# Hybrid trunk on one core: the first norm's squares summed on TensorE, v's last pass by chunks, the meta product over 128 rows, and other matmul costs in the planner

## The chip, the core and the metric

The kernel runs on one core of a Trainium2 chip. A core has a matrix engine (TensorE; PE in the profile, its weight loads PEld), a vector engine (VectorE, DVE), a scalar engine (ScalarE, ACT), a general engine (GpSimd, POOL) and SyncE (SP), whose queue issues the DMAs here. The metric is the device time of one execution in microseconds; less is better.

## The reference

A decoder trunk of two layers over 528 tokens of width 1024: 16 learned meta tokens, then 512 tokens of the input. Each layer is, cut to what the change touches:

```python
xn = rms_norm(h, norm1_g[l])          # h * rsqrt(mean(h*h) + 1e-6) * g
proj = xn @ w_in[l]
z, xbc, dt_raw, q, k, v, gate_logits = jnp.split(proj, split_at, axis=-1)
y_ssd = ssd_mixer(z, xbc, dt_raw, ...)           # dt = softplus(dt_raw + dt_bias); chunks of 128
y_attn = sliding_window_attention(q, k, v, ...)  # 16 q heads, 4 kv heads of 64
merged = g_ssd * (y_ssd @ w_ssd_down[l]) + g_attn * (y_attn @ w_attn_down[l])
h = h + merged @ w_o[l]
hn = rms_norm(h, norm2_g[l])
h = h + jnp.square(jax.nn.relu(hn @ w_mlp_up[l])) @ w_mlp_down[l]
```

In the attention each block of 128 queries sees a window of 128 keys, all 16 meta tokens and a sink logit: `out = probs[..., :16] @ v_meta + probs[..., 16:] @ v_band`. The states of the SSD decay by `exp(cumsum(dt * a))`. All inputs are 32-bit floats, and the meta tokens are dropped from the output.

## The kernel before

**Layout.** The activations `h` lie with the 1024 features on partitions, as eight tiles (`KD` = 8) of 128 features by 528 tokens; the tokens are cut into five `CHUNKS`, of which chunk 0 holds the meta tokens. Every large product is made in three passes over numbers split in two, in a type of which TensorE takes a column at a time: weights into `whi` and `wlo` (ACT casts `whi`, POOL subtracts to get `wlo`, some of it DVE), activations into `hnh` and `hnl` (`hgh` and `hgl` in layer 1, where the norm's factor is put in later). The passes are high by high, low by high and high by low. Small products (sums over partitions, transposes, broadcasts) are made with plain 32-bit operands; TensorE's records show two of them for each.

**The start.** The eight tiles of `h`, the constants `cst` and the first weights are loaded. For the first norm ACT squares tile after tile, DVE adds all but the last square up in `acc`, and TensorE sums `acc` and the last square over the partitions with a column of ones: five chunks by two, ten products of 128 by 1 into one bank (`rms_tok`, from L592). DVE scales the sums, POOL raises them to the power of -1/2 (`rt`), TensorE broadcasts `rt` to all partitions (`bcast_tok`), DVE multiplies `h` by it, ACT and DVE make `hnh` and `hnl`. The later norms use the same functions.

**v and dt.** The first projection makes v (256 columns) and dt (32) together, 288 columns with the tokens as rows: five banks, one for each chunk, weights `wvh` and `wvl` (`WideWeights`, from L448). The first two passes go row by row (tile k by `wvh`, all five chunks, then the low part of the tile before); the last is

```python
for k in range(KD):
    v_row(k, 2, stop=k == KD - 1)      # wvl: for every k, all five chunks
```

so all five banks are finished together. Then each chunk is evicted in turn: `dtx` (DVE), the high part of v (ACT), the low part (DVE), into `vm` for the meta tokens and `vt` for the rest. `vm` is 64 rows: 32 rows, of which 16 count, and a copy of them. `dt_task` (L757) follows: a chain of 2 operations of ACT and 15 of DVE on 128 by 160 (`scr`, `dtx`, `dtt`) makes softplus and then `adt`, which TensorE sums along the tokens (`cst,adt`).

**Attention.** For each group of four heads and block of queries the scores are made, the largest taken (`mx`), exponentials and their sum made, and then `piece` (L1064) runs for each piece of the keys: TensorE transposes the probabilities (`cst,at`, L434), ACT copies them as the high part into `ar`, DVE subtracts to get the low part, and TensorE multiplies both by v. For the meta tokens high and low part are stacked in 64 rows, 32 each, so that there is one product of 64 by 512 (`ar,vm`); the other pieces take two of 128 by 512 (`ar,vt`).

**What sets the order.** The program is written out by a planner, `Flow` (L124). Tasks are generators in queues (weights, post, misc, chunk, attn, tail and others); each yields where it waits for data, a bank, or TensorE. The planner keeps a clock for every engine, adds to it the estimated cost of each instruction that it emits (`Engine.cost` for DVE, ACT and POOL, `mm` for TensorE), and between the large products (`tick`) lets those tasks step whose needs are met by its own clocks. The order so found is fixed for each engine; semaphores hold it at run time. For the matmuls the estimate is:

```python
if rhs.dtype == F32R and n >= 256:
    cost = n / 2.4
else:
    cost = max(n, 128) * 4 / 2.4 * (0.66 if o.shape[0] == 64 else 1.0)
```

`F.force` steps tasks until the given ones are done; `F.finish` and `F.step` move single tasks on. The conversion of v's first weights (the casts to `wvh` on ACT) is such a task, and was stepped twice, which issues the loads. There are eight banks of PSUM (`ps`), and two buffers each of `raw`, `xh`, `sq` and `zs`.

Of the kernel before, what the change touches and what calls it, by code (L numbers as in the profile page):

```python
# [9 lines left out]
F32 = mybir.dt.float32  # L10
F32R = mybir.dt.float32r
# [6 lines left out]
P = 128  # L18
# [288 lines left out]
class Engine:  # L307
# [12 lines left out]
    def cost(self, name, n, k, aps):  # L320
        scalars = sum(isinstance(k.get(x), bass.AP) for x in ("scalar", "scale", "bias", "mul"))
        if self._k == "v":
            if name == "reciprocal":
                return 6.4 * n + 60.0
            if name == "tensor_tensor_reduce":
                return n / 0.96 + 165.0
            return n / 0.96 + 62.0 + (58.0 if scalars else 0.0)
        if self._k == "s":
            psum = any(x.space == PSUM for x in aps)
            return n / 1.2 + (48.0 if psum else 86.0) + 93.0 * scalars + (95.0 if "accum_out" in k else 0.0)  # L330
        if k.get("op") == ALU.pow:
            return 190.0 * n + 120.0
        if name == "memset":
            return 40.0
        return n * (2.09 if name == "tensor_tensor" else 3.8) + 125.0
# [19 lines left out]
def hybrid_trunk_kernel(ctx: ExitStack, tc: tile.TileContext, h0, params, consts, rope, wdt, w, out,  # L355
# [69 lines left out]
    def mm(o, lhsT, rhs, start=True, stop=True):  # L425
        n = Engine.size(rhs)
        if rhs.dtype == F32R and n >= 256:
            cost = n / 2.4
        else:
            cost = max(n, 128) * 4 / 2.4 * (0.66 if o.shape[0] == 64 else 1.0)  # L430
        F.run("pe", cost, [o], [lhsT, rhs], PE.matmul(out=o, lhsT=lhsT, rhs=rhs, start=start, stop=stop))  # L431
# [160 lines left out]
    def rms_tok(sq, inv_n, cs, tag, rows=(), bank="ps"):  # L592


        yield {bank: 1, "after": rows, "data": lambda: [x[:, CHUNKS[cs[0]][0]:sum(CHUNKS[cs[-1]])] for x in sq()]}
        ps = Slot("ps")
        for c in cs:
            t0 = CHUNKS[c][0]
            x = sq()
            for i in range(len(x)):  # L600
                mm(ps.t[:, c:c + 1], x[i][:, t0:t0 + P], C("ones"), start=i == 0, stop=i == len(x) - 1)
# [3 lines left out]
        V.tensor_scalar(out=x, in0=ps.t[:, cs[0]:cs[-1] + 1], scalar1=inv_n, scalar2=EPS, op0=ALU.mult, op1=ALU.add)  # L605
        ps.free()
# [68 lines left out]
    for x, q in ((wt[0, "v", 0], "w"), (wt[0, "v", 1], "w"), (wvt.dt, "misc")):  # L675
        assert x in tasks_
        F.step(x, F.queues[q])
        F.step(x, F.queues[q])
# [4 lines left out]
    acc = Slot("zs", "acc")  # L683
    for k in range(KD):
        sq = Slot("sq") if k else acc
        S.activation(out=sq.t, in_=h(k), func=AF.Square)
        if k == KD - 1:
            nrm["sq"] = sq
        elif k:
            V.tensor_tensor(out=acc.t, in0=acc.t, in1=sq.t, op=ALU.add)  # L690
            sq.free()
    first.append(F.put("misc", norm(acc, 0, (), keep=True)))
    F.force(first)
    F.end = 0.0

    for l in range(depth):
# [130 lines left out]
        vm = lay.tile([64, NKV, 2, 64], F32R, name="vm", tag="vm")  # L827
# [6 lines left out]
        def v_row(k, x, start=False, stop=False):  # L834
            for c in range(5):
                t0 = CHUNKS[c][0]
                mm(banks[c].t[:, 0:wvt.N], (src.lo if x == 1 else src.hi)(k)[:, t0:t0 + P], wvt(1 if x == 2 else 0, k),
                   start=start, stop=stop)
# [8 lines left out]
        for k in range(KD):  # L847
            v_row(k, 2, stop=k == KD - 1)
        F.finish(*first)
        del first[:]  # L850
        for c in range(5):
            ps = banks[c]
            F.end = 0.0
# [148 lines left out]
        def attention(n, kv):  # L1002
# [61 lines left out]
            def piece(p):  # L1064
# [10 lines left out]
                if kk < P <= nq:  # L1075
# [12 lines left out]
                    mm(po[0].t[:, :4 * nq], vm[:, kv].rearrange("p x d -> p (x d)"), ar[0:64, h_],  # L1088
# [62 lines left out]
        ar = unit("ar", F32R).rearrange("p r t -> p (r t)")  # L1151
        put_attention(qt, 0)
# [571 lines left out]
```

## Time and profile before

| | |
|---|---|
| time of three runs, median (lowest to highest) | 2446.96 us (2444.26 to 2449.26) |
| time of the profiled execution | 2436.77 us |
| its span, first to last instruction | 2435.1 us |
| granted TensorE clock, mean over the span | 0.992 |
| busy: TensorE, DVE, ACT, POOL | 2363.5, 1337.1, 1025.4, 1097.8 us (97, 55, 42, 45% of the span) |
| moved by DMA | 257.33 MB, 106 GB/s on average |

The profiled execution lies 10.2 us under the median of the three timed ones and 7.5 us under the fastest. Times in the trace count from the span's start. TensorE's matmuls overlap, and the end of each is modelled, so what one costs in a row of like ones is read from the distance of two starts (the pitch), not from its length. [...] In brackets behind a row stands the engine's idle time before it, and who ended it.

### The profile page before, as it was taken

To read this page: it belongs to the slowest core of one execution; us is meant where nothing else is said; L and a number is where in the kernel's file an instruction comes from. 1 tells how busy PE (TensorE), PEld (TensorE's weight loads), DVE (VectorE), ACT (ScalarE), POOL (GpSimd) and SP (SyncE) were. 2 spreads that over 40 slices of the span, in tenths; PEclk is the share of its full clock that TensorE was granted. 3 is DMA by queue.
4 is the path that set the end of the run, shared out by engine and by line. 5 is a ranking of instruction groups with operands and counts; after the bars stand their busy time and mean duration, and the time that the engine had idled before them with its cause. 6 is when DMAs were issued, how large, how long until landed. Compare 5 with 4: busy or idle time off the path is not lost.

```text
span 2435.1 us, 40407 instructions
## 1 busy us (share of the span) xinstructions
PE 2363.5 (97%) x16038; PEld 2143.3 (88%) x16038; DVE 1337.1 (55%) x2509; ACT 1025.4 (42%) x1999; POOL 1097.8 (45%) x651
## 2 busy tenths in 40 slices
PE   6999999999999999999999899999999999999999
PEld 6889899999999999999997788888988788888887
DVE  5787788787522444233246868787875135433221
ACT  4365566564432233222244456556554223333231
POOL 3534434465444334343434454445555543444443
PEclk9999999999999999999999999999999999999999
DMA  4323333343443322222232233324434533222222
GB/s 138 91 75 106 83 102 93 90 116 101 118 177 113 141 79 87 96 87 96 94 136 82 69 100 105 106 73 121 118 93 133 177 121 135 89 95 95 95 95 104
DMA packets 133578, 257.33 MB, mean 106 GB/s; under 512 B 16470, under 2 KB 66318, under 8 KB 133390
## 3 DMA queue, kind: packets, MB, share of 16 engines
q1 hardware_dynamic: 133390, 254.75, 33.4%
q8 instruction: 127, 2.08, 0.3%
q14 instruction: 61, 0.50, 0.1%
HBM read 232.03 MB, written 17.33 MB: 102 GB/s over the span
## 4 chain that ended last, share of the span: by engine, by line
PE 80%; DVE 12%; issue 3%; ACT 2%; POOL 2%; DMA 1%; SPq 0%; DVEq 0%; POOLq 0%; ACTq 0%
PE ps L431 78%; PE ps L434 2%; DVE xb L348 2%; DVE at L348 1%; DVE raw L348 1%; DVE xh L348 1%; DVE rqs L348 1%; DVE scr L348 1%; DVE gm L348 1%; POOL wlo L348 1%; DVE ar L348 1%; DVE mx L348 1%; DMA gm<-ac_dram 0%; DVE qa L348 0%; ACT at L348 0%
## 5 line engine op out<-in xcount | busy, mean ns | idle before, releaser
L348 POOL TENSOR_TENSOR wlo<-wraw,whi 128x1024 fp32r<-128x1024 f32 x328 | 797.5, 2431 | 982.7 <-ACT whi L348 930.4
L348 ACT CAST whi<-wraw 128x1024 fp32r<-128x1024 f32 x340 | 355.5, 1046 | 707.5 <-PE ps L431 421.4
L431 PE MATMUL ps<-hnh,whi 128*128 128x266 f32 (+2 forms) x2048 | 401.2, 312 | 5.3 <-DVE vm L348 4.6
L431 PE MATMUL ps<-hnl,whi 128*128 128x266 f32 (+2 forms) x2048 | 399.3, 311 | 0.0
L431 PE MATMUL ps<-hnh,wlo 128*128 128x266 f32 (+2 forms) x2048 | 391.8, 308 | 0.0
L431 PEld LDWEIGHTS ps<-hnh,whi 128*128 128x128 f32 x2048 | 307.2, 192 | 20.6 <-issue 6.8
L431 PEld LDWEIGHTS ps<-hnl,whi 128*128 128x128 f32 x2048 | 307.7, 192 | 15.1 <-issue 1.3
L431 PEld LDWEIGHTS ps<-hnh,wlo 128*128 128x128 f32 x2048 | 304.0, 190 | 15.2 <-issue 2.3
L348 DVE SCALAR_TENSOR_TENSOR h<-ps,h 128x264 f32<-128x264 f32 (+1 forms) x120 | 62.1, 517 | 308.8 <-PE ps L431 308.8
L348 DVE TENSOR_TENSOR hidl<-s,hidh 128x528 fp32r<-128x528 f32 (+1 forms) x64 | 116.9, 1827 | 88.1 <-ACT s L348 88.1
L431 PE MATMUL ps<-hgl,whi 128*128 128x264 f32 (+1 forms) x768 | 153.7, 322 | 1.3 <-DVE hgl L348 1.3
L431 PE MATMUL ps<-hgh,wlo 128*128 128x264 f32 (+1 forms) x768 | 153.4, 321 | 0.0
L431 PE MATMUL ps<-hgh,whi 128*128 128x264 f32 (+1 forms) x768 | 152.8, 321 | 0.0
L431 PE MATMUL ps<-hidl,whi 128*128 128x264 f32 (+1 forms) x768 | 152.6, 321 | 0.0
L431 PE MATMUL ps<-hidh,whi 128*128 128x264 f32 (+1 forms) x768 | 152.5, 320 | 0.0
L431 PE MATMUL ps<-hidh,wlo 128*128 128x264 f32 (+1 forms) x768 | 152.5, 320 | 0.0
L431 PE MATMUL ps<-y,whi 128*128 128x264 f32 (+1 forms) x768 | 137.0, 320 | 0.0
L431 PEld LDWEIGHTS ps<-hgl,whi 128*128 128x128 f32 x768 | 119.0, 188 | 12.4 <-DVE hgl L348 1.6
L431 PEld LDWEIGHTS ps<-hgh,wlo 128*128 128x128 f32 x768 | 119.5, 189 | 11.0
L431 PEld LDWEIGHTS ps<-hidl,whi 128*128 128x128 f32 x768 | 118.9, 188 | 11.0
L431 PEld LDWEIGHTS ps<-hidh,wlo 128*128 128x128 f32 x768 | 118.8, 188 | 11.0
L431 PEld LDWEIGHTS ps<-hidh,whi 128*128 128x128 f32 x768 | 118.7, 188 | 11.1
(218 smaller groups left out, 3947.5 us busy)
## 6 DMA issues: line engine op xcount, KB each, us to landing
wraw<-w_dram SPq DMA_DIRECT2D x344, 512.0 KB
gm<-ac_dram SPq DMA_DIRECT2D x64, 256.0 KB
et<-ac_dram SPq DMA_DIRECT2D x128, 64.0 KB
t<-au SPq DMA_DIRECT2D x48, 66.0 KB
h<-h_dram SPq DMA_DIRECT2D x8, 264.0 KB
at<-rope_dram SPq DMA_DIRECT2D x4, 528.0 KB
y_dram<-xb SPq DMA_DIRECT2D x4, 528.0 KB
yr<-y_dram SPq DMA_DIRECT2D x8, 264.0 KB
```

What stands on the lines that cost most here:

```text
L348: inst = fn(*a, **k)
L431: F.run("pe", cost, [o], [lhsT, rhs], PE.matmul(out=o, lhsT=lhsT, rhs=rhs, start=start, stop=stop))
L434: F.run("pe", 108.0 if in_.shape[1] > 64 else 60.0, [o], [in_], PE.transpose(out=o, in_=in_, identity=C("ident", k)[:, :k]))
```

## The change

1. **The first norm's sums.** DVE adds nothing up any more. Each of the eight squares goes to TensorE as it is made: five products of 128 by 1 for each, 40 instead of ten, into five banks. The squares take turns in four kinds of buffer. The five sums are then scaled on DVE one by one. The casts to `wvh` are stepped on right behind the norm. ACT's order at the start of the program, before (`acc` is the buffer of the first square and of the sum):

```order
L348 ACTIVATE acc<-h_80 128x528
L348 ACTIVATE sq<-h_80 128x528 x3
L348 ACTIVATE sq<-h_81 128x528 x4
L348 ACTIVATE hnh_154<-h_80,par 128x528 x2
L348 CAST wvh<-wraw 128x7x128
L348 CAST wvh_93<-wraw 128x128
L348 CAST wvh<-wraw 128x7x128
L348 CAST wvh_93<-wraw 128x128
L348 CAST wvh<-rawdt 128x7x32
L348 CAST wvh_93<-rawdt 128x32
L348 ACTIVATE hnh_154<-h_80,par 128x528 x2
```

And after:

```order
L350 ACTIVATE sq<-h_80 128x528 x4
L350 ACTIVATE sq<-h_81 128x528 x4
L350 CAST wvh<-wraw 128x7x128
L350 CAST wvh_93<-wraw 128x128
L350 CAST wvh<-wraw 128x7x128
L350 CAST wvh_93<-wraw 128x128
L350 CAST wvh<-rawdt 128x7x32
L350 CAST wvh_93<-rawdt 128x32
L350 ACTIVATE hnh_192<-h_80,par 128x528 x4
L350 ACTIVATE hnh_193<-h_81,par 128x528
```

The casts to `wvh` stood behind the first two `hnh` and stand ahead of them now.

2. **v's last pass by chunks.** The products with `wvl` run chunk by chunk, eight for each, and each chunk's eviction follows its own. 40 products before, 40 after. `vm` becomes 128 rows, the upper 64 filled with zeros by POOL once a layer.

3. **The meta product.** It reads 128 rows of `ar` and `vm` instead of 64; the upper rows of both `ar` buffers are filled with zeros by POOL, once a layer. The products of the 16-row meta block stay as they were.

4. **The planner's costs.** A large product counts n/2.25 + 4 ns instead of n/2.4 (121 instead of 110 for 264 columns), a small one n * 4/2.28 instead of n * 4/2.4, a product with an output of 64 rows 0.9 of that instead of 0.66; on DVE the product with a running maximum (`tensor_tensor_reduce`) counts 25 ns more, and a `tensor_scalar` without PSUM about half. This moves instructions on all engines. On TensorE in layer 0, in the large products for k and q that follow v, around the decay's first sums (`cst,adt`), before:

```order
L431 MATMUL ps<-hnh_155,wlo 128x264 x2
L431 MATMUL ps<-hnh_154,whi 128x264 x4
L431 MATMUL ps<-cst,adt 32x128 x4
L431 MATMUL ps<-hnh_155,whi 128x264 x2
L431 MATMUL ps<-hnl_156,whi 128x264 x4
L431 MATMUL ps<-hnl_157,whi 128x264 x2
L431 MATMUL ps<-cst,au 128x2 x5
L431 MATMUL ps<-hnh_154,wlo 128x264 x2
L431 MATMUL ps<-cst,adt 32x16
L431 MATMUL ps<-adt,cst 16x32
```

And after:

```order
L433 MATMUL ps<-hnl_195,whi 128x264 x2
L433 MATMUL ps<-hnh_193,wlo 128x264 x2
L433 MATMUL ps<-hnh_192,whi 128x264 x4
L433 MATMUL ps<-hnh_193,whi 128x264 x2
L433 MATMUL ps<-hnl_194,whi 128x264 x4
L433 MATMUL ps<-hnl_195,whi 128x264 x2
L433 MATMUL ps<-hnh_192,wlo 128x264 x2
L433 MATMUL ps<-cst,adt 32x128 x4
L433 MATMUL ps<-hnh_192,wlo 128x264 x2
L433 MATMUL ps<-hnh_193,wlo 128x264 x2
```

The decay's `cst,adt` stood behind the 124th large product after v (of 264 columns) and five sums `cst,au`; it stands behind the 62nd now. In the attention of layer 1 the same holds for a group of probabilities. TensorE, the 79th of 92 groups, from its transposes to its product with v, before:

```order
L434 MATMUL ps<-cst,at_14821 128x128 x4
L431 MATMUL ps<-hnl_14181,whi 128x512 x4
L431 MATMUL ps<-xdd,btk 128x256
L431 MATMUL ps<-hnl_14182,whi 128x512 x2
L434 MATMUL ps<-cst,xb 128x128 x3
L431 MATMUL ps<-xb 128x128
L431 MATMUL ps<-hnh_14179,wlo 128x512 x4
L431 MATMUL ps<-hnh_14180,wlo 128x512 x2
L431 MATMUL ps<-hnh_14180,whi 128x512 x2
L431 MATMUL ps<-hnl_14182,whi 128x512 x2
L431 MATMUL ps<-hnh_14180,wlo 128x512 x2
L431 MATMUL ps<-ar,vt 128x512 x2
```

And after:

```order
L436 MATMUL ps<-cst,at_14856 128x128 x4
L433 MATMUL ps<-hnl_14218,whi 128x266 x2
L433 MATMUL ps<-hnl_14219,whi 128x266 x2
L433 MATMUL ps<-hnh_14216,wlo 128x266 x4
L433 MATMUL ps<-hnh_14217,wlo 128x266 x2
L433 MATMUL ps<-hnh_14217,whi 128x266 x2
L433 MATMUL ps<-hnl_14219,whi 128x266 x2
L433 MATMUL ps<-hnh_14217,wlo 128x266 x2
L433 MATMUL ps<-hnh_14216,whi 128x266 x2
L433 MATMUL ps<-ar,vt 128x512 x2
```

Between the transposes and the product stood 18 products of 512 columns and five smaller instructions, and there stand 18 of 266 columns now. Over all 92 groups the distance shrinks in more than half and grows in the others. Over the whole program DVE takes 21 subtractions of the split of q instead of 8, and POOL 15 instead of 28.

The diff, cut:

```diff
@@ -323,7 +323,9 @@
...
             if name == "tensor_tensor_reduce":
-                return n / 0.96 + 165.0
+                return n / 0.96 + 190.0
+            if name == "tensor_scalar" and not any(x.space == PSUM for x in aps):
+                return n / 1.92 + 62.0 + (58.0 if scalars else 0.0)
             return n / 0.96 + 62.0 + (58.0 if scalars else 0.0)
...
@@ -425,9 +427,9 @@
     def mm(o, lhsT, rhs, start=True, stop=True):
         n = Engine.size(rhs)
         if rhs.dtype == F32R and n >= 256:
-            cost = n / 2.4
+            cost = n / 2.25 + 4.0
         else:
-            cost = max(n, 128) * 4 / 2.4 * (0.66 if o.shape[0] == 64 else 1.0)
+            cost = max(n, 128) * 4 / 2.28 * (0.9 if o.shape[0] == 64 else 1.0)
...
@@ -589,21 +591,25 @@
-    def rms_tok(sq, inv_n, cs, tag, rows=(), bank="ps"):
-        yield {bank: 1, "after": rows, "data": lambda: [x[:, CHUNKS[cs[0]][0]:sum(CHUNKS[cs[-1]])] for x in sq()]}
-        ps = Slot("ps")
-        for c in cs:
-            t0 = CHUNKS[c][0]
-            x = sq()
-            for i in range(len(x)):
-                mm(ps.t[:, c:c + 1], x[i][:, t0:t0 + P], C("ones"), start=i == 0, stop=i == len(x) - 1)
+    def rms_tok(sq, inv_n, cs, tag, rows=(), bank="ps", sums=None):
+        if not sums:
+            yield {bank: 1, "after": rows, "data": lambda: [x[:, CHUNKS[cs[0]][0]:sum(CHUNKS[cs[-1]])] for x in sq()]}
+            ps = Slot("ps")
+            for c in cs:
+                t0 = CHUNKS[c][0]
+                x = sq()
+                for i in range(len(x)):
+                    mm(ps.t[:, c:c + 1], x[i][:, t0:t0 + P], C("ones"), start=i == 0, stop=i == len(x) - 1)
         yield
         r = sm.tile([P, 5], F32, name=tag, tag=tag)
         x = r[:, cs[0]:cs[-1] + 1]
-        V.tensor_scalar(out=x, in0=ps.t[:, cs[0]:cs[-1] + 1], scalar1=inv_n, scalar2=EPS, op0=ALU.mult, op1=ALU.add)
-        ps.free()
+        for c in cs if sums else (cs[0],):
+            y, z = (x[:, c:c + 1], sums[c].t[:, 0:1]) if sums else (x, ps.t[:, c:cs[-1] + 1])
+            V.tensor_scalar(out=y, in0=z, scalar1=inv_n, scalar2=EPS, op0=ALU.mult, op1=ALU.add)
+        for z in sums or (ps,):
+            z.free()
@@ -672,7 +678,8 @@
...
-    for x, q in ((wt[0, "v", 0], "w"), (wt[0, "v", 1], "w"), (wvt.dt, "misc")):
+    v_tasks = ((wt[0, "v", 0], "w"), (wt[0, "v", 1], "w"), (wvt.dt, "misc"))
+    for x, q in v_tasks:
         assert x in tasks_
         F.step(x, F.queues[q])
         F.step(x, F.queues[q])
@@ -680,17 +687,30 @@
...
-    acc = Slot("zs", "acc")
+
+    sums = [Slot("ps") for _ in CHUNKS]
     for k in range(KD):
-        sq = Slot("sq") if k else acc
+        sq = Slot(min(("zs", "sq", "xh", "raw"), key=lambda n: F.rings[n].at()), "sq")
         S.activation(out=sq.t, in_=h(k), func=AF.Square)
-        if k == KD - 1:
-            nrm["sq"] = sq
-        elif k:
-            V.tensor_tensor(out=acc.t, in0=acc.t, in1=sq.t, op=ALU.add)
-            sq.free()
-    first.append(F.put("misc", norm(acc, 0, (), keep=True)))
+        for c in range(5):
+            t0 = CHUNKS[c][0]
+            mm(sums[c].t[:, 0:1], sq.t[:, t0:t0 + P], C("ones"), start=k == 0, stop=k == KD - 1)
+        F.end = F.t["pe"]
+        sq.free()
+
+    def first_norm():
+        nrm["rt"] = yield from rms_tok(None, 1.0 / D, range(5), "rt", sums=sums)
+        nrm["banks"] = []
+        for x in bcast_tok(nrm["rt"], range(5), "bank"):
+            if isinstance(x, dict):
+                yield x
+            else:
+                nrm["banks"].append(x)
+
+    first.append(F.put("misc", first_norm()))
     F.force(first)
+    for x, q in v_tasks:
+        F.step(x, F.queues[q])
...
@@ -824,18 +844,18 @@
...
-        vm = lay.tile([64, NKV, 2, 64], F32R, name="vm", tag="vm")
+        vm = lay.tile([P, NKV, 2, 64], F32R, name="vm", tag="vm")
+        G.memset(vm[64:128].bitcast(F32), 0.0)
         rtm = sm.tile([32, 1], F32, name="rtm", tag="rtm")
         rows_, src = (made, hg) if l else (normal, hn)
         F.force(rows_[:2])
         F.finish(wvt.dt, wt[l, "v", 0], wt[l, "v", 1])
         banks = [Slot("ps") for _ in CHUNKS]
 
-        def v_row(k, x, start=False, stop=False):
+        def v_row(k, x, start=False):
             for c in range(5):
                 t0 = CHUNKS[c][0]
-                mm(banks[c].t[:, 0:wvt.N], (src.lo if x == 1 else src.hi)(k)[:, t0:t0 + P], wvt(1 if x == 2 else 0, k),
-                   start=start, stop=stop)
+                mm(banks[c].t[:, 0:wvt.N], (src.lo if x else src.hi)(k)[:, t0:t0 + P], wvt(0, k), start=start, stop=False)
                 F.tick()
 
         for k in range(KD + 1):
@@ -844,12 +864,14 @@
                 v_row(k, 0, start=k == 0)
             if k:
                 v_row(k - 1, 1)
-        for k in range(KD):
-            v_row(k, 2, stop=k == KD - 1)
         F.finish(*first)
         del first[:]
         for c in range(5):
             ps = banks[c]
+            for k in range(KD):
+                t0 = CHUNKS[c][0]
+                mm(ps.t[:, 0:wvt.N], src.hi(k)[:, t0:t0 + P], wvt(1, k), start=False, stop=k == KD - 1)
+                F.tick()
             F.end = 0.0
...
@@ -1085,7 +1107,7 @@
...
-                    mm(po[0].t[:, :4 * nq], vm[:, kv].rearrange("p x d -> p (x d)"), ar[0:64, h_],
+                    mm(po[0].t[:, :4 * nq], vm[:, kv].rearrange("p x d -> p (x d)"), ar[:, h_],
                        start=(p == 0), stop=(p == len(pieces) - 1))
...
@@ -1149,6 +1171,8 @@
 
         at2 = unit("at2").rearrange("p r t -> p (r t)")
         ar = unit("ar", F32R).rearrange("p r t -> p (r t)")
+        for i in range(2):
+            G.memset(ar[64:128, i * 1024:i * 1024 + 512].bitcast(F32), 0.0)
```

## Rows read from the trace of the kernel before

**Rows 1.** The page, part 1: each engine's busy time, share, instructions

```profile
PE 2363.5 (97%) x16038; PEld 2143.3 (88%) x16038; DVE 1337.1 (55%) x2509; ACT 1025.4 (42%) x1999; POOL 1097.8 (45%) x651
```

**Rows 2.** Waits, TensorE: who waited <- for whom: total us, times, longest

```profile
PE ps L431 <- DVE ar L348: 17.2, 15, 2.3
...
PE ps L431 <- DVE mx L348: 6.5, 1, 6.5
```

**Rows 3.** Chain that ended last, 0 to 30 us: start, length, what

```profile
5.31 5.00 DMA cst<-consts_dram
...
24.57 2.36 ACT wvh L348 x5
...
26.97 3.25 PE ps L431 x12
```

**Rows 4.** Timeline, 13 to 46 us: start, length, engine, operation; TensorE, then ACT

```profile
14.98 0.56 PE L431 MATMUL ps<-cst,acc 128*128 128x1 f32 x2
...
17.97 0.57 PE L431 MATMUL ps<-cst,sq 128*128 128x1 f32 x2
...
31.93 1.38 PE L431 MATMUL ps<-wvh,hnl 128*128 128x288 f32 x5
...
33.13 0.83 PE L431 MATMUL ps<-wvh,hnh 128*128 128x288 f32 x5
...
40.45 5.45 PE L431 MATMUL ps<-wvl,hnh 128*128 128x288 f32 x40
...
23.16 1.41 ACT L348 ACTIVATE hnh<-h,par 128x528 fp32r<-128x528 f32 x2 [8.67 <-DVE h L348]
```

**Rows 5.** Busy time by stretch (window, its length, each engine, clock)

```profile
core 0: us, PE busy (x) PEld busy (x) DVE busy (x) ACT busy (x) POOL busy (x), PEclk, DMA share, GB/s
879.66:883.07 3.41, 3.41 (x31) 3.41 (x32) 0.17 (x1) 0.00 (x0) 1.03 (x1) 1.00 0.43 153
883.07:886.49 3.42, 3.42 (x17) 3.15 (x16) 0.02 (x1) 0.39 (x1) 0.15 (x1) 0.50 0.00 0
```

**Rows 6.** Timeline inside the first stretch, TensorE: the last of ten sums

```profile
881.40 0.36 PE L431 MATMUL ps<-cst,sq 128*128 128x1 f32 x2
```

**Rows 7.** Timeline of layer 0's decay chain: DVE, POOL, TensorE

```profile
49.95 0.18 DVE L348 TENSOR_TENSOR dtx<-ps,par 128x32 f32<-128x32 f32 x1
...
51.46 0.24 DVE L348 TENSOR_SCALAR scr<-scr 128x160 f32<-128x160 f32 x1 [0.46 <-ACT scr L348]
...
52.93 2.87 DVE L348 TENSOR_TENSOR scr<-scr 128x160 f32<-128x160 f32 x2
...
64.78 0.32 DVE L348 TENSOR_TENSOR adt<-dtt,na 128x160 f32<-128x160 f32 x1
...
53.22 2.39 POOL L348 TENSOR_TENSOR wlo<-wraw,whi 128x1024 fp32r<-128x1024 f32 x1 [13.33 <-ACT whi L348]
...
65.16 1.06 PE L431 MATMUL ps<-cst,adt 128*32 128x128 f32 x8 [3.06 <-DVE adt L348]
```

**Rows 8.** Timeline of one attention step, TensorE

```profile
1368.92 0.50 PE L431 MATMUL ps<-ar,vm 64*128 64x512 f32 x1 [2.25 <-DVE ar L348]
...
1369.35 0.66 PE L434 MATMUL ps<-cst,at 128*128 128x128 f32 x4
...
1371.70 0.62 PE L431 MATMUL ps<-ar,vt 128*128 128x512 f32 x2
...
1372.16 0.41 PE L431 MATMUL ps<-hnh,whi 128*128 128x266 f32 x2
```

**Rows 9.** Timeline, layer 1's first norm and first k product, TensorE

```profile
1264.43 0.36 PE L431 MATMUL ps<-cst,acc 128*128 128x1 f32 x2
...
1265.99 0.36 PE L431 MATMUL ps<-cst,sq 128*128 128x1 f32 x2
...
1268.25 1.03 PE L431 MATMUL ps<-cst,rt 16*128 16x16 f32 x6
...
1280.11 1.00 PE L431 MATMUL ps<-hnh,whi 128*128 128x264 f32 x3 [4.57 <-DVE vm L348]
```

## The prediction

> **What bounds the kernel now.** I read the page's busy shares first: TensorE is busy for 2363.5 of 2435.1 us, the next engine for 1337.1 [rows 1]. So there are two ways to win: fewer or cheaper matmuls, or less of the roughly 72 us in which TensorE stands still. The waits of TensorE came second: it waited 17.2 us in 15 places for DVE's half of the split probabilities (`ar`), and once 6.5 us for the largest score of an attention group [rows 2]. Third, the chain of the start: until 10.31 us the constants are under way, and ACT's casts of v's weights (24.57 to 26.93) stand directly ahead of the first v product at 26.97 [rows 3]. The same stretch of the timeline shows that TensorE runs there at the lower of its two speeds: five v products take 1.20 us (31.93 to 33.13), and later 40 take 5.45 [rows 4].
>
> The profiled execution took 2436.77 us, 1.67 more than its span; I sum against it, and add the result to the median of 2446.96, which lies 10.2 us higher.
>
> **The change part by part.**
>
> *The start.* Removed from the path: six adds on DVE. Added: 30 more sums on TensorE. Eight sums are 2.99 us apart there (14.98 to 17.97, seven distances), 0.427 us each [rows 4]. The sums need the constants, which land at 10.31 [rows 3]; 40 of them last until 27.4, against 18.5 before: 8.9 us later. Behind them comes the same chain (scale, power, broadcast, multiply) to the first `hnh`, which ACT began at 23.16 and ended after half of 1.41 us, at 23.9 [rows 4]; now 32.8. But the casts to `wvh` no longer follow on that: ACT runs them while TensorE sums, so the first v product starts there and not after them. 32.8 against 26.97 is **+5.9 us**. One DVE operation became five small ones, which I count as nothing, because the distance of two small operations there is hidden in my rounding to 0.1 for each, at most +0.5. In the other direction the speed may rise sooner, since TensorE has worked longer: of the 25 v products that ran at 0.24 us before 33.13 half would then take 0.136, a gain of 1.3. Range +4.6 to +6.4.
>
> [...]
>
> *v's last pass by chunks.* The 40 products remain, at 0.136 us. What moves is the eviction. Before, v ends at 45.9, the five evictions follow on DVE and ACT, the last `dtx` starts at 49.95, and the decay chain's DVE part starts at 51.46, 5.6 us behind v [rows 4, 7]. Now four evictions run beside the products of the next chunks, and the chain starts 1.5 us (49.95 to 51.46) after the last one, so at about v's end + 1.6. The chain is 15 DVE operations: the first two take 1.47 us (51.46 to 52.93), the other 13 between 0.24 and 0.32 each when nothing disturbs (the first and the last of the chain), at most 4.2 us [rows 7]. So `adt` is ready at v's end + 7.3. Its first sums stand behind 62 large products instead of 124 and five sums: 62 times 0.125 (0.136 by 264 of 288 columns, an estimate) is 7.7 us. They would just not wait, where before they waited 3.06 us at 65.16 [rows 7]. I take **-2.8**. The other end: two operations of the chain took 2.87 us instead of 0.64 while POOL made a weight's low half from 53.22 on, and the whole chain took 13.6 us (51.46 to 65.10) [rows 7]. With that price in full, `adt` is ready at v's end + 15.2, and TensorE waits 7.5 us: +4.5. POOL's subtraction began 7.3 us behind v's end; the chain now ends about there. That is why I choose the undisturbed end, and why the other one is a rival. Low end -3.1.
>
> *The meta product.* 32 products of 64 rows by 512 columns. One starts 0.43 us ahead of what follows (1368.92 to 1369.35), a product of 128 rows with the same 512 columns 0.23 (1371.70 to 1372.16, two) [rows 8]. Taking the shape of the latter, each saves 0.20: **-6.3**. The upper rows are zeros and are written by POOL once a layer, three fills on an engine that is idle for more than half of the span [rows 1]. No row shows such a fill; the nearest, a subtraction of 128 by 1024, takes POOL 2.39 us [rows 7], and a fill has a quarter to a half of its elements. The weights' second buffer hides it; without that cover a layer would lose up to 2.4 us once. High end 0, if rows had nothing to do with it. [...] The two rows differ by a factor of 1.9, so the measurement decides.
>
> *Layer 1's entry.* There the planner, whose products are now dearer by a tenth, puts the norm's ten sums behind 49 products of v and no longer behind 63. TensorE then waits 4.57 us for a bank that only `vm`'s eviction frees, at 1280.11, and that eviction stands on DVE behind the rows that wait for the norm [rows 9]. Fourteen products of 0.136 us are 1.9 us by which the norm starts earlier in the same work. The chain from the sums to the broadcast (1266.2 to 1268.25) is covered by v products as before [rows 9]. I take **-1.6**, from 0 to -4.6, the whole wait.
>
> *The order in the attention.* The new costs make TensorE slower in the planner's book, by a tenth for large products, and DVE faster for copies, so it believes an `ar` to be ready after fewer products. Counting the work that stands on TensorE between a group's transposes and its product with v, at the pitches above, the median of 92 groups falls from 3.9 to 2.9 us, and those under 2.5 us rise from 18 to 32. A fixed latency of 2.6 us, beyond which each missing microsecond is waited for, gives 17.3 us before, which is what the waits show [rows 2], and 25.6 with the new order: +8.3. But DVE's and ACT's queues move with it: where the work came close, DVE was often late because of something else queued ahead. I take half, **+4**. Ends: +15 with a latency of 2.9 us (37.8 less 23.4, rounded up) and -5, if the 6.5 us pause [rows 2] falls to 1.5 in the new order and nothing else changes. In the order the products ahead of that pause are as many as before, so I let it stand.
>
> Thirteen subtractions of q's split go from POOL to DVE, which is 45% idle [rows 1]; nothing, or part of the last term.
>
> **Sum:** +5.9 - 2.8 - 6.3 - 1.6 + 4 = -0.8 us. 2436.8 becomes 2436.0; 2446.96 becomes **2446**.
>
> **The rivals.**
>
> 1. *The order costs nothing.* The groups that moved closer were ones whose DVE work was early, and the pause shrinks: the last part is -5 instead of +4, the sum -9.8, the time 2437. For it speaks that only 15 of 92 groups waited although 18 had less than 2.5 us; against it that the new order more than doubles the groups under 2.9 us (23 to 46).
> 2. *The sums raise the clock.* If 17 us of sums bring TensorE to the upper level, a sum costs 0.223 us as in layer 1 (1264.43 to 1265.99, seven distances) [rows 9]: 40 times 0.204 is 8.2 us less, and the first 25 v products save 2.6. Sum -11.6, 2435. Against it stands the stretch from 879.66 [rows 5].
> 3. *Slower: the decay chain meets POOL's subtraction.* If that starts 2 us earlier in the new order (ACT's casts are sooner done) or v's last eviction is late by as much, seven or more of the chain's operations run at several times their length. The price is 7.3 over my value, the sum +6.5, 2453.5. It decides from about 5 us behind v's end. For it: rows 7 show this very chain disturbed.
> 4. *Slower: the dense attention is paid in full,* by the latency of 2.9 us: +15 instead of +4, the sum +10.2, 2457.
> 5. *The meta product gains nothing,* because its time has another reason than its rows: sum +5.5, 2452.5.
>
> **How the numbers follow.** What a measurement of this kernel can tell from no change is about 0.2%, 4.9 us: 2442.1 to 2451.9. My forecast, 2446 with a range of its own from 2442 to 2451, has 0.34. Faster: rival 1 has 0.30, rival 2 0.08, together 0.38. Slower: rival 3 has 0.13, rival 4 0.10, rival 5 0.05, together 0.28. The range from 2434 to 2458 takes in all five; a start that runs as fast as rival 2 together with rival 1, or rivals 3 and 4 together, would lie outside.
>
> **What the profile would show.** The start: last sum at about 27, `wvh` casts done before it, first v product near 32.8; pitch of the sums 0.43 (0.22 for rival 2). The decay: `cst,adt` without a wait worth the name some 8 us behind v's end; with 7 us of waiting for `adt`, rival 3. The meta product: 0.23 from start to next start in 32 places. Layer 1: the wait for `vm` near 3 us instead of 4.57. Attention: waits for `ar` between 17 and 26 us in total, more than 15 of them. I am wrong in kind if TensorE's stall outside these places changes by more than 5 us, since I have followed the new order at these places alone, and the change moves instructions on all engines.

## The result: slower by 1.5%

The changed kernel took 2484.36 us in the median of four runs (2479.49 to 2489.51), the kernel before 2447.11 in four; the ratio is 1.0153, with a 95% interval from 1.0130 to 1.0176. The forecast was 2446 with a range up to 2458: the time lies above the range, and on the other side of the likeliest case.

The two profiled executions differ by more, 52.7 us (2436.77 and 2489.51), since that of before is faster than all its timed runs and that of the changed kernel the slowest of its four. Places are compared in these two; how much a kernel is worth is told by the medians. The page after, its span and the busy times (before: [rows 1]):

```profile
span 2487.7 us, 40502 instructions
PE 2392.4 (96%) x16098; PEld 2169.2 (87%) x16098; DVE 1343.1 (54%) x2524; ACT 1026.4 (41%) x1999; POOL 1078.2 (43%) x640
```

Where it went is seen when the trace is cut at the same places of the program: the first product of v, of k, of the branches' merge (which ends the mixers), of layer 1's v, of its k and of its merge. In us, length of each stretch:

| stretch | before | after |
|---|---|---|
| start to v's first product | 27.0 | 32.7 |
| layer 0: v | 18.8 | 19.7 |
| layer 0: k, q, mixers | 640.7 | 667.6 |
| layer 0: merge and MLP, up to layer 1's v | 569.3 | 569.2 |
| layer 1: v | 19.5 | 21.0 |
| layer 1: k, q, mixers | 619.1 | 636.7 |
| layer 1: merge and MLP | 536.8 | 537.0 |

The start costs what was forecast. 44.5 of the 52.7 us are in the mixers, where the planner mixes the large products with the small steps of attention and SSD. The view of busy times by stretch shows the two mixers; before first (columns: stretch, its length, busy time and count by engine, granted clock, DMA share, GB/s):

```profile
core 0: us, PE busy (x) PEld busy (x) DVE busy (x) ACT busy (x) POOL busy (x), PEclk, DMA share, GB/s
45.70:686.50 640.80, 622.10 (x4954) 585.40 (x4953) 480.71 (x1074) 346.65 (x835) 311.62 (x220) 0.99 0.34 98
1275.30:1894.30 619.00, 593.34 (x3822) 512.03 (x3822) 460.02 (x967) 327.28 (x711) 303.69 (x216) 0.98 0.35 100
```

And after:

```profile
core 0: us, PE busy (x) PEld busy (x) DVE busy (x) ACT busy (x) POOL busy (x), PEclk, DMA share, GB/s
52.40:720.00 667.60, 629.78 (x4953) 592.49 (x4952) 491.06 (x1084) 344.70 (x831) 292.19 (x209) 0.97 0.33 94
1310.20:1946.90 636.70, 600.10 (x3823) 517.30 (x3822) 455.73 (x969) 326.58 (x712) 298.47 (x214) 0.97 0.33 97
```

TensorE's idle time in them (length less busy) rose from 18.7 and 25.7 us to 37.8 and 36.6. Its busy time rose too, by 7.7 and 6.8 us, though the meta product got cheaper: the granted clock fell from 0.99 and 0.98 to 0.97. By the trace's clock records the two mixers spent 68 us at a granted clock of 0.50 instead of 34; that is some 17 us of work at half the clock (an estimate). The longest such stretch: TensorE waits 3.95 us from 117.4 on (k and q, held by DVE), and the clock falls at 120.6 and stays low for 17.1 us; the view of busy times around it:

```profile
117.10:120.60 3.50, 0.33 (x3) 0.12 (x2) 3.29 (x7) 0.00 (x0) 2.22 (x2) 1.00 0.44 150
120.60:137.70 17.10, 15.32 (x69) 14.60 (x70) 10.84 (x40) 5.48 (x25) 4.10 (x2) 0.50 0.16 48
```

In the trace after, large products of 264 columns follow each other in 0.220 us at a granted 0.50 and in 0.121 at 1.00 (medians). At half the clock the 15.32 busy us cost about 7.7 more than at full (an estimate), twice the wait itself. The price varies: in the same execution a wait of 3.77 us that ended at 1318.30 is followed by 3.4 us at 0.50 (from 1318.67).

Who TensorE waited for (who waited, for whom, total us, times, longest). Before, beside [rows 2]:

```profile
PE ps L431 <- POOL xdd L348: 1.5, 3, 0.9
```

And after:

```profile
PE ps L433 <- DVE ar L350: 22.7, 18, 2.9
PE ps L433 <- POOL xdd L350: 11.7, 13, 2.6
...
PE ps L433 <- DVE gm L350: 6.4, 5, 2.2
PE ps L433 <- DVE mx L350: 6.4, 1, 6.4
PE ps L433 <- ACT hnh L350: 6.0, 4, 3.8
PE ps L433 <- DVE q L350: 4.4, 2, 3.9
```

`ar` rose by 5.5 us. POOL's `xdd` (an SSD chunk's inputs, scaled for its state) rose from 1.5 us in 3 places to 11.7 in 13, and I had not looked at it.

### The profile page after: what moved, and what is told of

The parts are those of the page before. It is cut to its first block, busy times and chain, and to the rows that moved or that the text cites. A ratio compares the mean times of both kernels' runs of the same rounds, so it can differ in the third digit from the quotient of the medians.

```text
span 2487.7 us, 40502 instructions
## 1 busy us (share of the span) xinstructions
PE 2392.4 (96%) x16098; PEld 2169.2 (87%) x16098; DVE 1343.1 (54%) x2524; ACT 1026.4 (41%) x1999; POOL 1078.2 (43%) x640
## 5 line engine op out<-in xcount | busy, mean ns | idle before, releaser
L433 PE MATMUL ps<-hnh,wlo 128*128 128x266 f32 (+2 forms) x2048 | 399.7, 312 | 0.0
L433 PEld LDWEIGHTS ps<-hnh,whi 128*128 128x128 f32 x2048 | 306.6, 193 | 18.8 <-ACT hnh L350 4.7
L350 DVE SCALAR_TENSOR_TENSOR raw<-ps,half,raw 128x265 f32<-128x265 f32 (+2 forms) x240 | 117.5, 490 | 22.8 <-ACT raw L350 17.0
```

The lines of the kernel that those rows point to most:

```text
L350: inst = fn(*a, **k)
```

## Which part of the change does it

Theory A: the planner's costs make the loss, through the order. Theory B: the start and the v pass do, since they shift every clock in the plan. First the changed kernel with the costs of before, in short:

```diff
-            cost = n / 2.25 + 4.0
+            cost = n / 2.4
```

and the other three costs likewise.

> The changed kernel with the four planner costs of before (parts 1 to 3 of the change stay). Theory A, the costs make the loss: the mixers go back to about 640 and 619 us (changed kernel 668 and 637), the start keeps its +5.7 us, the meta product its -6; the time is within 4 us of the kernel before, about 2445. Theory B, the three other parts make it, since a start that ends later and a v pass by chunks shift every engine's clock in the plan: the mixers stay near 668 and 637, the time near 2484.

Measured: 2430.27 us, ratio to before 0.9935 (0.9913 to 0.9957). Mixers 625.8 and 616.3 us. Parts 1 to 3 together make the kernel *faster* by 0.65%. Theory B falls; theory A has the direction, but its 2445 is missed too, by 15 us.

The counterpart, the four new costs put into the kernel before:

> The kernel before with the four new planner costs and nothing else. Theory A: the mixers are some 25 and 18 us longer than before, less nothing for the meta product, so about 2447 + 43 = 2490. Theory B: 2447, within 5 us.

Measured: 2486.57 us, 1.0166 (1.0145 to 1.0187); mixers 686.3 and 624.1. The total is near theory A's 2490, the places are not: the mixers grew by 45.6 and 5.0 us, where 25 and 18 were expected. Then the costs of matmuls and of DVE apart (first and second pair of the diff's lines):

> The kernel before with the two new costs of matmuls only. Theory A1, the matmul costs (a tenth more for large products) take away a slack that the too low cost gave every waiting step: most of the loss, 2475 to 2490. Theory A2, the two DVE costs do it (copies are believed ready too soon): within 5 us of 2447.

> The kernel before with the two new DVE costs only. Theory A1: within 8 us of 2447. Theory A2: 2470 to 2490.

Measured: 2496.27 us, 1.0200 (1.0178 to 1.0223), and 2447.04 us, 1.0004 (0.9993 to 1.0015). The costs of matmuls are to blame, by somewhat more than I expected; those of DVE alone change nothing (on top of the matmul costs they win 9.7 us, 2496.27 to 2486.57).

Large and small products apart:

> The kernel before with the new cost of the large products only (n/2.25 + 4). Slack theory: the too low cost of before made the planner put about a tenth more products between a step and its use than its own estimates asked for, and that hid latencies that it does not count; taken away, the two mixers lose together some 35 us: 2475 to 2495. Rival, the small products' cost (0.9 for 64 rows) is to blame: within 8 us of 2447. Rival, chance (any new order is as likely to be worse by this much): no statement.

> The kernel before with the new cost of the small products only. Slack theory: the small products are few, a tenth or less of TensorE's time in the mixers; 0 to +12, so 2445 to 2459. Rival: 2475 and more.

Measured: 2479.10 us, 1.0144 (1.0117 to 1.0171), and 2431.98 us, 0.9954 (0.9934 to 0.9974). The large products' cost is the culprit. The small ones' alone makes the kernel 0.5% faster, outside what I expected, and put on top of the large ones' it makes it slower by 17 us (2479.1 to 2496.3): the effects don't add up, so a part of what an order costs belongs to that order alone.

The parts by themselves:

> The kernel before with the meta product over 128 rows and nothing else. Prediction's term: 32 products from 0.43 to 0.23 us, -6.3, 2439 to 2441. Rival, that the waits beside it take the gain back: within 2 us of 2446.

Edit: `vm` and `ar` with 128 rows, the upper ones filled with zeros. Measured: 2437.36 us, 0.9971 (0.9957 to 0.9984), 7.3 us less than the kernel before in the same runs. The order on TensorE, DVE and ACT is that of before; POOL has six fills more. In the traces the 32 meta products stand 13.9 us ahead of what follows them before, summed, and 9.3 with 128 rows: 4.7 of the 7.3 us are the product's own, and the rest lies within the interval (3.9 to 10.5 us).

> The kernel before with v's last pass by chunks and nothing else. If this part made most of what the old costs with all three parts won in layer 0's mixer (640.7 to 625.8 us, of which 3.2 are the meta product's): mixer near 629, layer 1's entry some 3 us longer, time 2434 to 2439. If the gain came from the shifted start and its luck in the order: within 4 us of 2446.

```diff
-        for k in range(KD):
-            v_row(k, 2, stop=k == KD - 1)
+            for k in range(KD):          # in the loop over the chunks, ahead of the eviction
+                mm(ps.t[:, 0:wvt.N], src.hi(k)[:, t0:t0 + P], wvt(1, k), start=False, stop=k == KD - 1)
```

Measured: 2431.35 us, 0.9947 (0.9928 to 0.9966): 13.3 us less, more than expected. Layer 0's mixer takes 631.0 us instead of 640.7.

## How the large products' cost does it

The first idea was a slack. The trace of before has 0.122 us from one large product of 264 columns to the next (the median; 0.232 for 512 columns); the old cost says 0.110, the new one 0.121. So the new cost is nearly right, and the old one made the planner put a tenth more products between a step and its use than its own estimates of the other engines asked for. If that distance hides latencies, the loss goes with the cost:

> The kernel before, large products counted at 0.95 times the old cost, so still farther from their measured spacing. Slack theory: more distance between steps and their use, fewer waits: no slower than before, 2437 to 2448. Rival, that a cost nearer to the measured one is better in itself: slower than before. Chance: anywhere.

> The kernel before, large products counted at 1.05 times the old cost. Slack theory: between before and the full new cost (1.10), 2452 to 2470. Chance: anywhere from 2435 to 2495, and not in line with 0.95 and 1.10.

```diff
-            cost = n / 2.4
+            cost = n / 2.4 * 1.05      # or 0.95
```

Measured: 2436.67 us at 0.95 (ratio 0.9970, 0.9954 to 0.9985) and 2461.40 us at 1.05 (1.0073, 1.0052 to 1.0094). With 2444.6 for the old cost (before, in these runs) and 2479.10 for the full new one: 2437, 2445, 2461, 2479, in the order of the cost, as the idea has it.

One place that goes with it is in the SSD chunks. In each chunk ACT makes `gm` (its decay matrix) and copies `btk` (its B, transposed by TensorE), DVE makes `xdt` (the inputs times dt), POOL scales that to `xdd`, and TensorE multiplies `xdd` by `btk`. The timeline of the changed kernel around 456 us, in order of time:

```profile
453.83 0.49 PE L436 MATMUL ps<-cst,xb 128*128 128x128 f32 x3
...
455.70 0.66 PE L433 MATMUL ps<-gm,xdt 128*64 128x128 f32 x8
...
456.40 0.38 SPq L230 DMA_DIRECT2D gm<-ac_dram  x1
...
456.94 1.28 ACT L350 ACTIVATE gm<-gm,acs 128x128 f32<-128x128 f32 x4 [3.80 <-DMA gm<-ac_dram]
...
458.13 0.24 ACT L350 COPY btk<-ps 128x128 f32<-128x128 f32 x1
...
458.40 0.42 DVE L350 TENSOR_TENSOR xdt<-ps,dtt 128x256 f32<-128x256 f32 x1 [2.15 <-ACT btk L350]
...
458.90 0.61 POOL L350 TENSOR_TENSOR xdd<-xdt,ddt 128x256 f32<-128x256 f32 x1 [5.31 <-DVE xdt L350]
...
459.57 0.70 PE L433 MATMUL ps<-xdd,btk 128*128 128x256 f32 x2 [2.32 <-POOL xdd L350]
```

This is a ring. TensorE's products with `gm` (to about 456.3) free the buffer; SP loads the next `gm` at 456.40; ACT, which had been idle for 3.80 us, works it up; `btk`, ready for ACT since the transposes of 453.83, stands behind that in ACT's queue; `xdt` on DVE and `xdd` on POOL follow, and TensorE, which has run out of products ahead of `xdd,btk`, waits 2.32 us. From the end of the `gm` products to `xdd,btk` the ring takes 3.3 us. The same rows stand around 509 us, with a wait of 2.63, and around 562 us (with two more operations of ACT between `gm` and `btk`), with one of 3.04, which the profile puts down to ACT's `whi`; these three are the longest ahead of `xdd,btk`.

That `gm` stands shortly ahead of `btk` is not new: within four operations of ACT it does in 27 of 64 places before and in 25 after, but TensorE waits in 2 of those before and in 8 after. What shrank is the work that TensorE has from the transposes to `xdd,btk`: in the quarter of the places where it is least, it is at most 2.5 us at 0.95, 2.3 before, 1.9 at 1.05, 1.6 at the full cost alone and 1.4 in the changed kernel (counted at the traces' pitches, an estimate; the medians, in the same order 3.9, 3.4, 3.9, 3.3 and 3.0 us, follow the cost less well). The waits of TensorE at 0.95 and at the full new cost alone:

```profile
PE ps L431 <- DVE ar L348: 17.7, 14, 2.5
...
PE ps L431 <- POOL xdd L348: 0.2, 1, 0.2
```

```profile
PE ps L431 <- DVE ar L348: 18.6, 19, 3.4
PE ps L431 <- POOL xdd L348: 14.0, 12, 3.9
...
PE ps L431 <- DVE adt L348: 10.0, 2, 6.7
```

`xdd` rises with the cost, most of it in one step: 0.2 us at 0.95, 1.5 before, 12.6 at 1.05, 14.0 at the full cost. So it does not carry the 18 us from 1.05 to the full cost; there the wait for `adt` rises from 4.2 to 10.0. `ar`, on which I had put the price of the order, does not rise in these four: 17.7, 17.2, 16.0, 18.6. It does with the dear costs on three other kernels: from 13.0 (`old_costs`) to 22.7 in the changed kernel, from 12.9 (`small_cost`) to 22.6 (`pe_costs`), and from 13.2 to 21.2 on `no_sums` below.

If distance is what is missing, it should be possible to give it back in another way, with all the new costs left in: the planner's allowance between two steps of a task (`LAT`, `LATP`).

> The changed kernel, with the planner's allowance between the end of a step and the next step of its task raised from 100 to 400 ns (both for steps that need TensorE and for others), all costs as in the changed kernel. Slack theory, that the true cost of the large products took away distance which hid latencies: this gives distance back, some half of the loss or more is won, 2450 to 2468. Rival, the dear cost does its harm otherwise (queues chosen differently, chance): 2478 to 2495.

Measured: 2459.10 us, 25 us won back of the 54 that the costs take from `old_costs` (2430.27); the wait for `xdd` falls from 11.7 to 1.4 us, the one for `ar` stays (23.5).

> The changed kernel with the allowance at 700 ns instead of 100 (late_steps had 400 and took 2459). Distance theory: still better or the same, 2440 to 2460. Rival, that 400 happened to give a good order: back towards 2484, 2470 and more.

Measured: 2446.02 us, ratio to before 1.0001 (0.9989 to 1.0014), 38 of the 54 us. The times are as the distance theory has them, the place is not. TensorE's waits for `xdd` at 400 and at 700 ns:

```profile
PE ps L433 <- POOL xdd L350: 1.4, 3, 0.9
```

```profile
PE ps L433 <- POOL xdd L350: 6.7, 11, 0.9
```

From 400 to 700 the kernel wins 13 us while this wait comes back; layer 0's mixer grows (641.4 to 653.6 us) and layer 1's shrinks (623.4 to 604.3). The work ahead of `xdd,btk`, counted as above, is 1.4 us at 100 ns, 1.7 at 400 and 2.6 at 700, so the wait does not follow it here. These two runs show that a larger allowance wins time back; that it does so by distance at this place they do not show.

## A kernel that beats both, and where the theory ends

Of the four parts, two cost time: the matmul costs and the sums at the start. The kernel `no_sums` leaves both out, and steps the casts to `wvh` on ahead of the first norm:

```diff
+    for x, q in v_tasks:
+        F.step(x, F.queues[q])
     first.append(F.put("misc", norm(acc, 0, (), keep=True)))
```

> The kernel before with v's last pass by chunks, the meta product over 128 rows and the casts to wvh stepped ahead of the first norm; the first squares are summed on DVE and the costs are those of before. If the sums on TensorE cost what the trace of the changed kernel says (last sum ends at 27.3 us against 18.5), the first v product starts near 24 us, against 33.1 with the sums and the old costs and 27.0 before; everything later as in that run: 2421 to 2425. If the start is hidden by something later, 2428 to 2432.

Measured: 2421.53 us, ratio to before 0.9904 (0.9887 to 0.9921). It beats both kernels, the changed one by 63 us. `old_costs` has the same order on TensorE but for the sums, so they cost the difference of the two, 8.7 us. ACT's and TensorE's timeline at its start:

```profile
14.44 2.16 ACT L348 CAST wvh<-wraw 128x896 fp32r<-128x896 f32 x4
16.50 0.49 ACT L348 CAST wvh<-rawdt 128x224 fp32r<-128x224 f32 x2
23.20 1.42 ACT L348 ACTIVATE hnh<-h,par 128x528 fp32r<-128x528 f32 x2 [6.21 <-DVE h L348]
```

```profile
18.02 0.56 PE L431 MATMUL ps<-cst,sq 128*128 128x1 f32 x2
...
23.99 2.77 PE L431 MATMUL ps<-wvh,hnh 128*128 128x288 f32 x10 [1.28 <-ACT hnh L348]
...
29.45 0.83 PE L431 MATMUL ps<-wvh,hnl 128*128 128x288 f32 x5
```

The casts run right behind the squares, while TensorE sums and POOL works, and `hnh` starts when it did before (23.16 in [rows 4]); v starts at 23.99, where it was 26.97. Its mixers, in the view by stretch:

```profile
43.70:672.10 628.40, 616.33 (x4953) 584.68 (x4952) 461.32 (x1068) 344.33 (x831) 312.43 (x225) 0.99 0.36 99
1264.10:1881.00 616.90, 589.98 (x3823) 510.62 (x3822) 459.96 (x967) 327.05 (x711) 304.71 (x218) 0.99 0.36 100
```

Idle 12.1 and 26.9 us, clock 0.99 in both. Now the large products' cost on this kernel, to both sides, and the allowance:

> no_sums with the large products counted at n/2.25 + 4, as in the change. Distance theory: the loss of about 35 us comes back on this kernel too: 2445 to 2465. Rival (the loss belonged to the order of one kernel): within 10 us of 2421.5.

> no_sums with the large products counted at 0.95 times the old cost. Distance theory: a little less waiting, 2410 to 2422, by what 0.95 gave the kernel before (some 8 us). Rival: 2430 and more.

> The fastest kernel so far (no_sums, old costs) with the planner's allowance between a task's steps raised from 100 to 400 ns. Distance theory: the old order still waits some 11 us for ar, and more distance hides it; no slower than 2421.5, 2400 to 2421. Rival, the old costs are a lucky order and any shift of the plan costs: 2430 to 2460.

Measured: 2467.39 us with the new cost, 46 more than without: the loss comes back on another kernel, with 14.8 us of waiting for `xdd` instead of 2.2 and 21.2 for `ar` instead of 13.2. But 0.95 gives 2439.21, and the allowance of 400 ns gives 2440.86, 18 and 19 us *slower* than `no_sums`. Here the distance theory fails as a general rule. TensorE's waits in `no_sums` and in `no_sums_late`:

```profile
PE ps L431 <- DVE ar L348: 13.2, 16, 2.2
...
PE ps L431 <- POOL xdd L348: 2.2, 2, 1.8
```

```profile
PE ps L431 <- DVE ar L348: 21.3, 16, 2.9
...
PE ps L431 <- POOL xdd L348: 2.2, 3, 1.4
```

`xdd` stays where it was, and `ar` rises from 13.2 to 21.3 us although by the count of the order the groups of `ar` stand farther from their use (median 4.7 us of work instead of 3.9, an estimate). So the distance in the order is not what holds `ar` here; what is queued ahead of it on DVE and ACT may be, and that I have not traced. What can be said is this: the dearer large products lose on all three kernels on which they were tried by themselves (before, by 17 us at 1.05 and 35 in full; with the small products' cost on, by 64; `no_sums`, by 46), and the waits for `xdd` account for 9 to 13 us in each. The rest is spread over other waits and the lower clock (granted over the span 0.983 in `large_cost`, 0.992 before; 0.986 in `no_sums_dear`, 0.992 in `no_sums`), and how the cost makes it stays open. Beside that, a new order is better or worse by up to some 20 us for reasons of its own. Layer 0's mixer is where most of that lies: 628.4 us in `no_sums`, 649.7 at 0.95, 647.1 with the allowance.

## The prediction, step by step

- **The start: right.** Forecast: last sum at 27.4 and v at 32.8; +5.9. The timeline of the changed kernel on TensorE:

```profile
10.10 17.20 PE L433 MATMUL ps<-cst,sq 128*128 128x1 f32 x80 [10.10 <-DMA cst<-consts_dram]
...
32.70 2.77 PE L433 MATMUL ps<-wvh,hnh 128*128 128x288 f32 x10 [1.28 <-ACT hnh L350]
...
39.05 0.82 PE L433 MATMUL ps<-wvh,hnh 128*128 128x288 f32 x5
...
47.16 5.43 PE L433 MATMUL ps<-wvl,hnh 128*128 128x288 f32 x40
```

 The 40 sums (80 records) last from 10.10 to 27.30, 0.43 us each, and v starts at 32.70: +5.7.
- **Rival 2, the sums raise the clock: wrong, as argued.** The sums stand 0.43 us apart to the end, where those of [rows 9] have 0.22, and the v products behind (from 32.70) 0.24 us where they follow each other, up to about 38.7, for 6.0 us, and 0.13 from there on; before, the 0.24 lasted from 26.97 to 33.15, 6.2 us. The clock records of the two traces begin at 38.7 and 33.15, with 1.00; none lies ahead of that, so for the start the pitch alone speaks. Over 17 us of sums it stayed as it was, and behind 6 us of v products it fell; nor did the 1.3 us come that the start's range had for a speed that rises sooner. The stretch from 879.66 that I argued from (1.00, and 0.50 in the stretch behind it, [rows 5, 6]) was thin evidence: TensorE had also waited 1.34 us just ahead of it, and beside the sums it ran large products.
- **The meta product: right in sign and mechanism, a little large.** In an attention step of layer 1 the product now stands 0.23 us ahead of the next, as in [rows 8] those with `vt`:

```profile
1496.19 0.39 PE L433 MATMUL ps<-ar,vm 128*128 128x512 f32 x1
1496.42 0.60 PE L436 MATMUL ps<-cst,at 128*128 128x128 f32 x4
```

 So it does in 18 of the 32 places; in the other 14 it stands 0.30 to 0.34 us ahead. That is 5.1 us less in the trace, for the 6.3 forecast; `vm_alone` measured 7.3 us less in time. 64 rows took 0.43 us here and 128 take 0.23 to 0.34.
- **v by chunks: right in sign, wrong in place and size.** The decay chain on DVE, POOL's subtraction and TensorE's product after the change:

```profile
54.65 0.24 DVE L350 TENSOR_SCALAR scr<-scr 128x160 f32<-128x160 f32 x1 [0.18 <-ACT scr L350]
...
57.19 2.48 DVE L350 SCALAR_TENSOR_TENSOR scr<-scr,scr 128x160 f32<-128x160 f32 x7
...
60.22 2.35 DVE L350 TENSOR_TENSOR adt<-dtt,na 128x160 f32<-128x160 f32 x1
```

```profile
59.91 2.47 POOL L350 TENSOR_TENSOR wlo<-wraw,whi 128x1024 fp32r<-128x1024 f32 x1 [11.48 <-ACT whi L350]
```

```profile
62.67 1.88 PE L433 MATMUL ps<-cst,adt 128*32 128x128 f32 x8 [2.50 <-issue]
```

 The chain starts sooner and runs undisturbed, as forecast, but for its last operation: `adt` took 2.35 us beside POOL's `wlo`, which began at 59.91 (0.32 without, [rows 7]). TensorE waited 2.50 us (the profile names "issue"; `adt` ended at 62.57) instead of 3.06: -0.6, not -2.8, a step towards rival 3. Alone (`chunks_alone`) TensorE waits 1.4 us there: -1.7. Yet the part alone is worth 13.3 us. About 10 of them are in layer 0's mixer, where the order is another one from the evictions on; the waits for `ar` there fall from 9.0 to 2.7 us, and why this order is better stays open.
- **Layer 1's entry: wrong.** The wait for `vm` fell from 4.57 to 1.23 us, but the next wait, for a row of `hnh` on ACT, grew from 0.73 to 3.77. Before, beside [rows 9]:

```profile
1286.68 0.52 PE L431 MATMUL ps<-hnh,whi 128*128 128x264 f32 x2 [0.73 <-ACT hnh L348]
```

 And after:

```profile
1311.72 0.61 PE L433 MATMUL ps<-hnh,whi 128*128 128x264 f32 x3 [1.23 <-DVE vm L350]
...
1318.30 0.53 PE L433 MATMUL ps<-hnh,whi 128*128 128x264 f32 x2 [3.77 <-ACT hnh L350]
```

 Together 5.0 instead of 5.3: the gain went to the next link. Before, DVE made seven of the norm's eight rows ahead of v's evictions and one behind them; now it makes six ahead and two behind (the evictions start at 1310.2, the next row at 1316.7), so `vm` comes one row sooner and `hnh` later.
- **The order: the step that failed.** For `ar` I had forecast +8.3, took half, and got +5.5 in the trace: that term was fair (against `old_costs`, where `ar` has 13.0 us, the costs add 9.7). But I had priced the order by that one wait and put all others at nothing, because I had followed the new order at a few places alone; I wrote that TensorE's stalls elsewhere would have to change by no more than 5 us. TensorE's idle time in the mixers rose from 44.4 to 74.4 us; of these 30 only 5.5 are `ar`'s, while the waits for `xdd` rose by 10.2, for `hnh` by 5.3, for DVE's `q` by 4.4 and for `gm` by 3.9. TensorE's busy time rose by another 14.5 us, net of what the meta product saved, with twice the time at a granted 0.50 (68 us, 34 before). Parts 1 to 3, for which I had summed -3.2 (+5.9 - 2.8 - 6.3), are worth -17 (`old_costs`, against 2446.95), and the costs, for which I had +2.4 (-1.6 for layer 1's entry and +4), are worth +54 (2430.27 to 2484.36).
- **Chance and range.** Rival 4 was the right direction with the wrong mechanism: it, too, priced `ar` alone. The range was drawn from terms that I had rows for; a change of the planner's costs moves hundreds of instructions, and the spread between orders, some 20 us either way here, should have stood in it.

## What to carry to other kernels

A planner's cost that is wrong can be load-bearing: here, making the large products' estimate right lost 35 to 64 us on three kernels, and part of that (9 to 13 us of waits for `xdd`) is work on TensorE that had covered the latencies of other engines. So a cost is measured apart from other edits, and the waits that it may have hidden are looked for, rings as the one above (buffer freed, load, in-order queue, next use) among them. Where an order is found by a planner, measure several neighbouring settings before one is called better: here neighbours differed by up to 20 us.

## What the hardware showed that I had not expected

A wait of TensorE can be paid twice: behind the one of 3.95 us that began at 117.4 the granted clock was 0.50 for 17.1 us, which cost about twice the wait again (an estimate); behind the one of 3.77 us that ended at 1318.30 it was 0.50 for 3.4 us. And 17.2 us of uninterrupted one-column sums stood 0.43 us apart to their end, where those of [rows 9] have 0.22; the pitch fell, from 0.24 to 0.13 us, behind some 6 us of the 288-column products that followed (in `no_sums` 5.5 us, from 23.99 to 29.45).
